# Value projection with its first two products ahead and in the same banks, and linear attention by token halves

## The chip, the cores and the metric

The kernel runs on one core of a Trainium2 chip. The metric is the device time of one execution in microseconds (us); smaller is better. The engines are TensorE (PE, with its weight loads shown apart as PEld), VectorE (DVE), ScalarE (ACT), GpSimd (POOL) and SyncE (SP), which here only issues transfers.

## The reference

Two layers are applied to 512 tokens of 2048 features. Each layer normalises the tokens, makes one wide input projection, runs two groups of heads on slices of it, gates their outputs, and projects back.

```python
D_MODEL, SEQ, DEPTH, CHUNK = 2048, 512, 2, 64
GLA_HEADS, GLA_DK, GLA_DV = 4, 128, 256      # linear attention
ATT_HEADS, ATT_HD = 8, 128                   # chunked attention

def gla_chunk_causal(q, k, v, log_a):        # by head: q, k are 512x128, v is 512x256
    L = cumsum(log_a) inside each chunk; L_end = its last row
    k_dec = k * exp(L_end - L)
    U = einsum('bnchk,bnchv->bnhkv', k_dec, v)          # one 128x256 matrix per chunk
    A = exp(L_end)
    S_c = A_c * S_{c-1} + U_c                           # scan over the 8 chunks
    return einsum('bnchk,bnhkv->bnchv', q * DK**-0.5, S)

def hybrid_layer(x, w_in, w_out, ...):
    h = rmsnorm(x, g_pre)
    gq, gk, gv, gg, ga, aq, ak, av, ag = split_columns(h @ w_in)
    log_a = log_sigmoid(ga @ w_alpha + b_alpha) / 16
    o_gla = rmsnorm(gla_chunk_causal(gq, gk, gv, log_a), per head) * silu(gg)
    o_att = rmsnorm(chunk_band_attention(aq, ak, av, rel_bias), per head) * silu(ag)
    y = concatenate([o_gla, o_att]) @ w_out
    return x + rmsnorm(y, g_post)
```

## The kernel before

**The large products.** The input projection is cut into blocks of 512 columns. The blocks go in pairs (b0, b1), and each pair is multiplied by a scheme of the Strassen kind: seven products P1 to P7 of half-size matrices. A product runs over four chunks c of the inner dimension; one product and one chunk is a `Job`. A job is 12 matmuls of 128x512: each weight is split into a high part `wh` and a low part `wl` (ACT casts `wh` in line L251, DVE makes `wl = src - wh` in L257), and the left operand is split likewise, with three of the four partial products taken, for two halves kk of the chunk and two tiles t of 128 tokens. The weight sources are blocks of 512 KB that arrive in `raw` and `H`; DVE adds or subtracts them for some products (L240 `H += raw`, L243 `raw = H - raw`, L263 `H += src`). All jobs of a layer stand in one list, `stream`; `ahead` prepares them three to five places before they are used, so that loads, casts and differences run beside the matmuls of earlier jobs. A job's matmuls are recorded under line L504 (feature-major pairs under L491, and plain, unpaired blocks, called std, under L380).

**How a pair comes to its four results.** `Pair` holds two PSUM banks X and two banks Y, each a tile of 128x512 per token tile t. In the plain order, `PROD`, the products run P1, P5, middle (P6 and P3 mixed), P7, P2, P4. ACT copies P1, P5 and P6 out of the banks into SBUF tiles `ev` (L430 with a scale per token, L432 without). A result is then a bank combined with such a kept copy by DVE (L445), or a bank alone, scaled and evacuated by ACT (L1397 where the consumer is the value pair). P2 goes into fresh banks Y, and DVE adds the kept P1; P4 continues the sum in X.

In the early form, which the three front pairs of a layer use, P1 and P2 run first. With `seeded`, P2 is added on top of P1 in the same banks X. ACT keeps a copy of P1 before that (L432), writes the copy back into X afterwards (`open`, L439), and once P7 has closed copies X into Y (L517), where P4 then adds up. A function of line L504 called `matmuls` orders a few of the jobs next to such copies by token tile, so that one bank closes ahead of the other (`by_tile`).

**The pairs of a layer.** After the front pairs come `PAIRS`: two pairs of attention queries and keys, then keys and queries of linear attention, then the value pair `PAIRS[3] = (GV0, GV1)`. The value pair is the stage of this study. It has 28 jobs, that is 336 matmuls. After it two std blocks of the output projection follow (the std stage), then an output pair in the early form.

**What runs between the matmuls.** Other work is written as generators in a list `tasks`; `pump` advances it by steps at a rate given to `run`, and `until` advances it as far as something needs. A scheduler then sets the order of instructions on each engine. Near the value pair this work is the last heads of attention and then linear attention. `gla_heads(j, gv)` does heads 2j and 2j+1 in four units, one per head and half of the tokens (4 chunks each), head by head: (2j, first half), (2j, second half), (2j+1, first half), (2j+1, second half). It is started when all of (GV column block j) is done. A unit does: `outer` (8 matmuls of PE per half, L1255, k and v of a chunk; half of the array), `states` (four steps of the scan on DVE, L1274 and L1276, into a tile of slot g9 or g10 by half), `read` (8 matmuls, L1289, half of the array), `norm` (sums of squares on ACT, L1299; the shift on ACT, L556; a power on POOL, L552), `gate` (two instructions of DVE, L1307), and five steps later `turn` (4 transposes on PE, L1317, ACT's scale, L1328, and a split). The names in lists of instructions are tiles: `mm` PSUM banks of large products, `ax` PSUM banks for the rest, `g_...` slots in SBUF, `sm` small columns, `sg` and `bias` the gate tiles.

Of the kernel before, what the change touches and what calls it, by code (L numbers as in the profile page):

```python
# [24 lines left out]
NB_IN = 14  # L25
# [10 lines left out]
def hybrid_trunk(  # L36
# [97 lines left out]
    PAIRS = ((QK01, QK23), (QK45, QK67), (GK, GQ), (GV0, GV1))  # L134
    W23 = (NB_IN + 2, NB_IN + 3)
    C_IN, C_END = (0, 1, 2, 3), (2, 3, 0, 1)
# [37 lines left out]
    class Job:  # L174
# [8 lines left out]
        def load(self):  # L183
            k, c, p, b0, b1 = self.kind, self.c, self.pair, self.b0, self.b1
            end = b0 == W23[0]
# [28 lines left out]
        def bring(self):  # L214
            k, c, p = self.kind, self.c, self.pair
            end = self.b0 == W23[0]
# [4 lines left out]
            if src is None or p.get("direct") or p.get("second") and (name, c) in RESIDENT:  # L221
                return
            until(lambda: (self.l, end, name, c) in made)
            if p.get("second"):
# [41 lines left out]
    for l in range(L):  # L266
# [139 lines left out]
    class Pair:  # L406
        def __init__(self, l, pair, consume, feature_major=False, early=False, end=False, scaled=True, seeded=False, keep=ev,
# [7 lines left out]
            self.by_tile = (("P7", C_IN[-1]), ("P4", C_IN[0]), ("P4", C_IN[-1]), ("P1", C_IN[-1]), ("P2", C_IN[0]))  # L415
# [6 lines left out]
            self.first, *_, self.last = C_END if end else C_IN  # L422
            self.acc, self.keep, self.kept = {}, {}, keep
# [53 lines left out]
        def matmuls(self, job, k, c):  # L477
# [18 lines left out]
            if not self.feature_major:  # L496
                order = [(kk, t) for kk in range(2) for t in range(2)]
                if self.seeded and (k, c) in self.by_tile:
                    order.sort(key=lambda z: z[1])
                for kk, t in order:  # L500
                    tok = slice(kk * 256 + t * P, kk * 256 + (t + 1) * P)
                    ops = ((0, job.wh), (0, job.wl), (1, job.wh))
                    for m, (part, rhs) in enumerate(ops):
                        nc.tensor.matmul(  # L504
# [3 lines left out]
                        )  # L508
            spent.add((self.l, LEFT.get(k), c))

        def run(self, prods, rate=0.0, skip=0, after=None):
            pace = Pace(rate, skip)
            for k, c in prods:
# [5 lines left out]
                ahead(held=int(k == "P7" and c == prods[prods.index((k, self.last)) - 1][1] and self.seeded))  # L519
# [284 lines left out]
    def output_sums(l, chunks):  # L804
# [10 lines left out]
        return make_sums(l, True, ("g0", "g1", "g2", "g3"), parts, chunks)  # L815
# [40 lines left out]
    def layer(l):  # L856
        last = l == L - 1
        if l:
            act_table("silu_and_others")
# [110 lines left out]
        def av_consume(j, h, t, src, comb):  # L970
# [15 lines left out]
            Pair(l, FRONT[0], gate_consume(1), scaled=False, **how),  # L986
            Pair(l, FRONT[1], gate_consume(0), scaled=False, x_bank=2, **how),
            Pair(l, FRONT[2], av_consume, keep=early_kept, close_p1=True, **how),
# [15 lines left out]
        front[0].open(0)  # L1004
# [3 lines left out]
        front[1].open(2)  # L1008
# [6 lines left out]
        front[2].open(0)  # L1015
# [21 lines left out]
        class Head:  # L1037
# [76 lines left out]
            def turn(self):  # L1114
                c, kk = self.hd // 2, self.hd % 2
                if kk == 0:
                    turned[c] = [slot(tag, [2, 512], F32R) for tag in ("g16", "g17")]
# [10 lines left out]
                for half in range(2):  # L1128
# [65 lines left out]
        fast_gemm(l, PAIRS[0], qk_consume(0), rate=2.1, feature_major=True, scaled=False, x_bank=0)  # L1194
        fast_gemm(l, PAIRS[1], qk_consume(1), rate=2.1, feature_major=True, scaled=False, x_bank=2)

# [35 lines left out]

        fast_gemm(l, PAIRS[2], kq_consume, rate=2.1, x_bank=0)

        gla_done = set()
        og = {}

        class Unit:
            def __init__(self, h, p, gv, prev):
                self.h, self.p, self.gv = h, p, gv  # L1240
                self.st = slot(f"g{9 + p}", [4, 256])
                self.prev = prev.st[:, 3, :] if p else None

            def outer(self):
# [6 lines left out]
                for tt in (1, 0):  # L1251
                    for cc in (1, 0):
                        r = slice(cc * 64, (cc + 1) * 64)
                        with tc.issue_after(mm) if mm else nullcontext():
# [3 lines left out]
                            ).ins  # L1258

            def states(self):  # L1260
                h, p = self.h, self.p
                tag = "sg" if (2 * h + p) % 2 else "bias"
# [6 lines left out]
                for q in range(4):  # L1269
                    n = 4 * p + q  # L1270
                    cur = self.st[:, q, :]
# [8 lines left out]
                    prev = cur  # L1280

            def read(self):
                h, p = self.h, self.p
                self.ps_o = aux()
                for tt in range(2):
                    for cc in range(2):
# [4 lines left out]
                            gqT[h // 2][:, h % 2, n * 64 : (n + 1) * 64], self.st[:, q, :],  # L1291
# [20 lines left out]
            def turn(self):  # L1312
# [264 lines left out]
```

## Time and profile before

| quantity | value |
|---|---|
| median of three runs | 1603.68 us (1603.67, 1603.68, 1607.72) |
| profiled execution, its own time | 1604.27 us |
| span of the profile | 1601.9 us |
| mean granted TensorE clock | 0.998 |
| read from memory over the span | 393.01 MB |
| value stage, layer 0 and layer 1 | 534.7 to 625.1 us, and 1327.3 to 1417.4 us |
| std stage up to the end of its second half, layer 0 and layer 1 | 625.1 to 681.3 us, and 1417.4 to 1474.0 us |

The span is what the profiler saw of the core; the execution's own time holds 2.37 us more around it. Rows of the profile have the engine, the line of the kernel, the operation, the tiles written and read, and the time; "idle" names what the engine waited for just before. A matmul's recorded duration overlaps its neighbour's, so the distance between the starts of two matmuls is what one costs.

### The profile page before, as it was taken

To read this page: it belongs to the slowest core of one execution; us is meant where nothing else is said; L and a number is where in the kernel's file an instruction comes from. 1 tells how busy PE (TensorE), PEld (TensorE's weight loads), DVE (VectorE), ACT (ScalarE), POOL (GpSimd) and SP (SyncE) were. 2 spreads that over 40 slices of the span, in tenths; PEclk is the share of its full clock that TensorE was granted. 3 is DMA by queue.
4 is the path that set the end of the run, shared out by engine and by line. 5 is a ranking of instruction groups with operands and counts; after the bars stand their busy time and mean duration, and the time that the engine had idled before them with its cause. 6 is when DMAs were issued, how large, how long until landed. Compare 5 with 4: busy or idle time off the path is not lost.

```text
span 1601.9 us, 24514 instructions
## 1 busy us (share of the span) xinstructions
PE 1588.1 (99%) x8818; PEld 1353.9 (85%) x8818; DVE 1258.1 (79%) x1580; ACT 924.1 (58%) x1534; POOL 189.1 (12%) x302
## 2 busy tenths in 40 slices
PE   9999999999999999999999999999999999999997
PEld 6787889999988887788887888899999888777886
DVE  6888887786877876778868989768778778866886
ACT  8565544456676544555685556445666765355543
POOL 1131000001101101310312100000000011013110
PEclk9999999999999999999999999999999999999999
DMA  9999966858868698799868899668588677979995
GB/s 373 358 337 347 337 220 247 306 188 288 296 216 282 219 345 302 274 376 335 346 241 333 305 345 334 228 228 306 187 312 281 223 263 248 352 241 351 367 330 214
DMA packets 150616, 467.82 MB, mean 292 GB/s; under 512 B 16492, under 2 KB 35956, under 8 KB 150496
## 3 DMA queue, kind: packets, MB, share of 16 engines
q1 hardware_dynamic: 127232, 385.79, 67.7%
q0 software_dynamic: 22688, 79.53, 13.0%
q8 instruction: 69, 1.13, 0.3%
q10 hardware_dynamic: 576, 0.95, 0.2%
q14 instruction: 51, 0.42, 0.1%
HBM read 393.01 MB, written 72.11 MB: 290 GB/s over the span
## 4 chain that ended last, share of the span: by engine, by line
PE 92%; issue 3%; DMA 2%; DVE 1%; POOL 1%; ACT 1%; SPq 0%; POOLq 0%; DVEq 0%
PE mm L504 49%; PE mm L491 20%; PE mm L380 11%; PE ax L1089 2%; PE ax L504 1%; PE ax L1072 1%; PE ax L1255 1%; PE ax L1289 1%; DMA raw<-in_w_dram 1%; DMA H<-in_w_dram 1%; PE ax L1051 1%; PE ax L1052 1%; PE ax L1050 1%; PE ax L687 0%; DVE wl L257 0%
## 5 line engine op out<-in xcount | busy, mean ns | idle before, releaser
L251 ACT CAST wh<-raw 128x1024 fp32r<-128x1024 f32 x256 | 269.3, 1053 | 234.0 <-PE mm L504 97.3
L257 DVE TENSOR_TENSOR wl<-raw,wh 128x1024 fp32r<-128x1024 f32 x256 | 312.5, 1221 | 114.9 <-PE mm L504 36.2
L251 ACT CAST wh<-H 128x1024 fp32r<-128x1024 f32 x239 | 251.1, 1053 | 211.7 <-PE mm L504 88.7
L257 DVE TENSOR_TENSOR wl<-H,wh 128x1024 fp32r<-128x1024 f32 (+1 forms) x241 | 292.9, 1217 | 91.1 <-PE mm L504 36.5
L504 PE MATMUL mm<-wh,sa 128*128 128x512 f32 x1088 | 345.2, 392 | 0.1
L504 PE MATMUL mm<-wh,g 128*128 128x512 f32 x832 | 258.1, 389 | 0.0
L504 PEld LDWEIGHTS mm<-wh,sa 128*128 128x128 f32 x1088 | 203.2, 188 | 43.3 <-issue 1.5
L491 PE MATMUL mm<-sa,wh 128*128 128x256 f32 x1280 | 235.9, 285 | 0.0
L504 PE MATMUL mm<-wh,a 128*128 128x512 f32 x704 | 228.8, 396 | 2.2 <-ACT a L113 0.9
L504 PE MATMUL mm<-wl,sa 128*128 128x512 f32 x544 | 212.6, 391 | 0.0
L240 DVE TENSOR_TENSOR H<-H,raw 128x1024 f32<-128x1024 f32 x160 | 194.3, 1220 | 17.5 <-DMA raw<-in_w_dram 9.4
L491 PEld LDWEIGHTS mm<-sa,wh 128*128 128x128 f32 x1280 | 199.4, 192 | 0.3
L504 PEld LDWEIGHTS mm<-wh,g 128*128 128x128 f32 x832 | 156.2, 188 | 32.3
L491 PE MATMUL mm<-sa,wl 128*128 128x256 f32 x640 | 181.0, 283 | 0.0
L504 PE MATMUL mm<-wl,g 128*128 128x512 f32 x416 | 162.3, 390 | 1.1 <-DVE wl L257 1.1
L504 PEld LDWEIGHTS mm<-wh,a 128*128 128x128 f32 x704 | 131.6, 188 | 35.4 <-issue 4.9
L504 PE MATMUL mm<-wl,a 128*128 128x512 f32 x352 | 137.9, 393 | 0.6 <-DVE wl L257 0.5
L491 PEld LDWEIGHTS mm<-sa,wl 128*128 128x128 f32 x640 | 122.3, 191 | 0.1
L504 PEld LDWEIGHTS mm<-wl,sa 128*128 128x128 f32 x544 | 102.2, 188 | 21.3 <-DVE wl L257 0.3
L552 POOL TENSOR_TENSOR sm<-sm,cst 128x4 f32<-128x4 f32 (+2 forms) x40 | 59.4, 1486 | 321.6 <-DVE sm L1449 128.0
L491 PE MATMUL mm<-a,wh 128*128 128x256 f32 x512 | 94.4, 285 | 0.0
L504 PEld LDWEIGHTS mm<-wl,g 128*128 128x128 f32 x416 | 78.1, 188 | 18.9 <-DVE wl L257 2.6
(208 smaller groups left out, 2272.0 us busy)
## 6 DMA issues: line engine op xcount, KB each, us to landing
raw<-in_w_dram SPq DMA_DIRECT2D x352, 512.0 KB, 5.5
sa<-S SPq DMA_DIRECT2D x128, 512.0 KB, 4.7
H<-in_w_dram SPq DMA_DIRECT2D x63, 512.0 KB, 5.6
S<-g POOLq DMA_DIRECT2D x32, 512.0 KB, 6.4
g<-S SPq DMA_DIRECT2D x32, 512.0 KB, 5.2
sa<-A SPq DMA_DIRECT2D x32, 512.0 KB, 6.1
oS<-g POOLq DMA_DIRECT2D x32, 512.0 KB, 5.8
sa<-oS SPq DMA_DIRECT2D x32, 512.0 KB, 5.0
```

The lines of the kernel that those rows point to most:

```text
L240: nc.vector.tensor_tensor(out=h, in0=h, in1=r, op=ALU.add)
L251: last_cast[0] = nc.scalar.copy(self.wh, src).ins
L257: last_low[0] = nc.vector.tensor_tensor(out=self.wl[:, kk, :], in0=self.src[:, kk, :], in1=self.wh[:, kk, :].bitcast(F32), op=ALU.subtract ...
L380: mm = nc.tensor.matmul(pss[o], a[:, part, t], rhs[:, kk, :], start=(i == 0 and kk == 0 and m == 0), stop=(i == n - 1 and kk == 1 and m == 2),
L491: nc.tensor.matmul(dst, lhs[:, kk, f], a[:, part, tok], start=(fresh and kk == 0 and m == 0 and ft % 2 == 0), stop=(c == self.last and kk ...
L504: nc.tensor.matmul(out_ps[t], a[:, part, tok], rhs[:, kk, :], start=(fresh and kk == 0 and m == 0), stop=(c == self.last and kk == 1 and m ...
L552: return nc.gpsimd.tensor_tensor(out=out_r, in0=v, in1=mhalf[:, : v.shape[-1]], op=ALU.pow).ins
L1050: nc.tensor.matmul(ps[:, :n], self.qh[:, t], self.kh[:, :n], start=True, stop=False)
L1051: nc.tensor.matmul(ps[:, :n], self.qh[:, t], self.kl[:, :n], start=False, stop=False)
L1052: nc.tensor.matmul(ps[:, :n], self.ql[:, t], self.kh[:, :n], start=False, stop=True)
L1072: nc.tensor.transpose(ps[:, j * P : (j + 1) * P], self.prob[i][:, j * P : (j + 1) * P], ident)
L1089: nc.tensor.matmul(o, self.pt[i][:, j * P : (j + 1) * P], av[hd // 4, j // 2][:, j % 2, (hd % 4) * P : (hd % 4 + 1) * P], start=(j == 0), ...
```

## The change

- The value pair takes the early, seeded form: P1 and P2 first, P2 added in P1's banks; then P5, middle, P7, P4. It is split in two calls of `run` with `open` between. P4 needs its lower block of b0 again, so four more weight blocks of 512 KB are loaded per layer. The result (0, 0) of the pair, which DVE made from two tiles, is now evacuated by ACT.
- Linear attention no longer goes head by head. As soon as one of the pair's four results (column block j, token half h) is complete, `gla_heads` is started for the two heads of j and this half alone. The results come in the order (0,0), (1,0), (1,1), (0,1). The state at the end of the first half of each head is kept in `ends`, a slot of its own (g3), and the state tiles g9 and g10 alternate by the order of issue.
- The slots of the four results are new, result (0, 0) needs only the first attention head to be done, and `early_sums` waits in addition until the states of all eight units are issued.
- The counts that change over the whole program: 8 more block loads (`raw`, 352 to 360), the additions of L240 160 to 168 and those of L263 32 to 24, DVE's combinations of L445 20 to 16, ACT's evacuations of L1397 4 to 8, scaled copies of L430 32 to 28, plain copies of L432 64 to 68, writes back into a bank of L439 8 to 12, and copies from bank to bank of L517 12 to 16. PE runs the same instructions in another order.

The diff also has a whole second form of the output projection, `paired_out`, with `by_bank` and everything under `paired`, `W01` and `OUT`. It runs only for layers in `PAIRED`, which is empty, so `flip` is 0 and none of it is built. It is left out here.

```diff
         for b0, b1 in PAIRS:
-            pr = {"early": False}
-            stream += [Job(l, k, c, b0, b1, pr) for k, c in PROD]
+            pr = {"early": b0 == GV0}
+            order = early_head(C_IN) + early_rest(C_IN) if pr["early"] else PROD
+            stream += [Job(l, k, c, b0, b1, pr) for k, c in order]
...
-        gla_done = set()
-        og = {}
+        og, issued = {}, {"outer": 0, "states": 0}
+        ends = slot("g3", [4, 256])
 
         class Unit:
-            def __init__(self, h, p, gv, prev):
-                self.h, self.p, self.gv = h, p, gv
-                self.st = slot(f"g{9 + p}", [4, 256])
-                self.prev = prev.st[:, 3, :] if p else None
+            def __init__(self, h, p, gv):
+                self.h, self.p, self.gv, self.i = h, p, gv, issued["outer"]
+                st = slot(f"g{9 + self.i % 2}", [4, 256])
+                self.st = [st[:, q, :] for q in range(4)]
+                if p == 0:
+                    self.st[3] = ends[:, h, :]
+                self.prev = ends[:, h, :] if p else None
...
-        def gla_heads(j, gv):
+        def gla_heads(specs):
             units = []
 
             def new(k):
-                h, p = 2 * j + k // 2, k % 2
-                units.append(Unit(h, p, gv, units[-1] if p else None))
+                h, p = specs[k]
+                units.append(Unit(h, p, [gv[h // 2, z] if (h // 2, z) in gv else None for z in range(2)]))
                 units[-1].outer()
...
-            for k in range(4):
-                if k < 3:
+            for k in range(len(specs)):
+                more = k < len(specs) - 1
+                if more:
                     new(k + 1)
...
         def early_sums():
             while not {(p, h) for p in range(2) for h in (2, 3)} <= set(og):
                 yield
-            yield from output_sums(l, (2,3,))
+            while not paired and issued["states"] < 8:
+                yield
+            yield from output_sums(l, (2, 3))
...
-        GV = {1: ("g4", "g5"), 0: ("g0", "g1")}
+        GV = {(0, 0): "g2", (1, 0): "g4", (1, 1): "g5", (0, 1): "g0"}
...
-                until(lambda: 4 in heads_done)
-                gv[j, h] = slot(GV[j][h], [2, 512])
+                until(lambda: (4 if j or h else 0) in heads_done)
+                gv[j, h] = slot(GV[j, h], [2, 512])
...
-            if h and t:
-                heads = gla_heads(j, [gv[j, p] for p in range(2)])
-                tasks.append(heads if j else beside(heads, early_sums(), 3))
-
-
-        fast_gemm(l, PAIRS[3], gv_consume, rate=4, after=fetch_operands, x_bank=2)
+            if t:
+                heads = gla_heads([(2 * j, h), (2 * j + 1, h)])
+                tasks.append(beside(heads, early_sums(), 3) if (j, h) == (0, 1) else heads)
+
+        values = Pair(l, PAIRS[3], gv_consume, early=True, seeded=True, x_bank=flip ^ 2)
+        values.run(early_head(C_IN), rate=4, after=fetch_operands)
+        values.open(flip ^ 2)
+        values.run(early_rest(C_IN), rate=4, after=fetch_operands)
```

In the order of instructions the two programs are the same up to the value pair of layer 0, and again in the stages behind the std stage; the same differences stand in layer 1. Two places show them.

**PE, inside linear attention.** Before, the last `outer` of column block 1 and the next `read` (both on half of the array) stand side by side near the end of the value pair. L504 rows are matmuls of the large product, L1255 is `outer`, L1289 is `read`.

```order
L504 MATMUL mm_5835<-wl_6183,a_46_374 128x512
L1255 MATMUL ax_6272<-g_1176_6084,g_1066_5576 128x256
L1255 MATMUL ax_6271<-g_1176_6084,g_1066_5576 128x256
L1255 MATMUL ax_6272<-g_1176_6084,g_1066_5576 128x256
L1255 MATMUL ax_6271<-g_1176_6084,g_1066_5576 128x256
L1289 MATMUL ax_6278<-g_1200_6204,g_1016_5341 64x256 x4
L504 MATMUL mm_5835<-wh_6166,a_46_374 128x512
L504 MATMUL mm_5715<-wh_6186,sa_6188 128x512
```

After, the reads of the first two units stand in pieces among the matmuls of the middle products (L517 is the large product there, L1320 is `read`; `g_1098` is `ends`).

```order
L517 MATMUL mm_5910<-wh_5931,sa_5933 128x512
L1320 MATMUL ax_5977<-g_1147_5935,g_1015_5340 64x256 x3
L1320 MATMUL ax_5977<-g_1098_5715,g_1015_5340 64x256
L1320 MATMUL ax_6018<-g_1151_5949,g_1015_5340 64x256 x2
L517 MATMUL mm_5910<-wl_5969,sa_5933 128x512
L517 MATMUL mm_5910<-wh_5931,sa_5933 128x512
L517 MATMUL mm_5911<-wh_5931,sa_5933 128x512
L517 MATMUL mm_5911<-wl_5969,sa_5933 128x512
L1320 MATMUL ax_6018<-g_1151_5949,g_1015_5340 64x256
L517 MATMUL mm_5911<-wh_5931,sa_5933 128x512
L1320 MATMUL ax_6018<-g_1098_5715,g_1015_5340 64x256
L517 MATMUL mm_5910<-wh_5931,sa_5933 128x512
```

Counted over the whole program, unbroken stretches of `outer` and `read` rows between two full-size matmuls are 24 before and 32 after; per layer two of the eight units move from the std stage into the value stage.

**ACT, at the turn from the last-but-one product to P4 of the value pair.** Before, ACT has the casts of P2 and P4 and the steps of linear attention (`norm` L1299 and L556, `turn` L1328) there.

```order
L251 CAST wh_6186<-H_5572 128x1024
L251 CAST wh_6226<-H_5607 128x1024
L1299 ACTIVATE t_1210_6243,sm_6241<-ax_6230 128x256
L1299 ACTIVATE t_1211_6245,sm_6241<-ax_6230 128x256
L556 ACTIVATE sm_6247<-sm_6241,cst 128x2
L251 CAST wh_6264<-H_5638 128x1024
L251 CAST wh_6297<-H_5668 128x1024
```

After, it also has the two copies from X to Y (L541) between the casts of P4 (L254), ahead of the `norm` of two units (L1330, L580).

```order
L254 CAST wh_6309<-H_5607 128x1024
L541 COPY mm_5912<-mm_5910 128x512
L254 CAST wh_6390<-H_5638 128x1024
L541 COPY mm_5913<-mm_5911 128x512
L1330 ACTIVATE t_1242_6336,sm_6334<-ax_6323 128x256
L1330 ACTIVATE t_1243_6338,sm_6334<-ax_6323 128x256
L580 ACTIVATE sm_6340<-sm_6334,cst 128x2
L1330 ACTIVATE t_1250_6368,sm_6366<-ax_6361 128x256
L1330 ACTIVATE t_1251_6370,sm_6366<-ax_6361 128x256
L254 CAST wh_6397<-H_5668 128x1024
L580 ACTIVATE sm_6372<-sm_6366,cst 128x2
```

P4's first matmuls in each bank Y now stand behind the copy into that bank, and the second copy stands behind the cast `wh_6390`.

Where a line of the kernel before has moved in the kernel after, the pairs that matter are: L504 and L517 (large product), L1255 and L1284 (`outer`), L1289 and L1320 (`read`), L1317 and L1348 (transposes), L1299 and L1330, L556 and L580, L552 and L576, L1307 and L1338 (`norm` and `gate`), L432 and L443, L439 and L450, L517 and L541, L445 and L456, L1397 and L1438 (copies and evacuations).

More of the change, by code (lines that the diff above doesn't have):

```diff
@@ L422, in __init__ @@
             self.first, *_, self.last = C_END if end else C_IN
+            self.by_tile = [(k, self.last) for k in ("P7", "P4", "P1")] + [(k, self.first) for k in ("P4", "P2")]
             self.acc, self.keep, self.kept = {}, {}, keep
@@ L475, in operand, with matmuls @@
             return S_on[self.l, LEFT[k], c]
-        def matmuls(self, job, k, c):
+        def matmuls(self, job, k, c, only=None):
             a = self.operand(job, k, c)
@@ L499, in matmuls @@
                     order.sort(key=lambda z: z[1])
+                if only is not None:
+                    order = [z for z in order if z[1] == only]
                 for kk, t in order:
@@ L508, in matmuls, with by_bank @@
                         )
+                self.closing = mm.ins
             spent.add((self.l, LEFT.get(k), c))
+        def by_bank(self, prods, evac):
+            jobs = [take(self.l, self.b0, k, c) for k, c in prods]
+            closing = None
+            for t in range(2):
+                for job, (k, c) in zip(jobs, prods):
+                    with tc.issue_after(closing) if closing else nullcontext():
+                        self.matmuls(job, k, c, only=t)
+                closing = self.closing
+                evac(t, self.acc[self.target[k]][t])
         def run(self, prods, rate=0.0, skip=0, after=None):
@@ L518, in run @@
                     last_evac[0] = seeds[0]
-                ahead(held=int(k == "P7" and c == prods[prods.index((k, self.last)) - 1][1] and self.seeded))
+                ahead(held=int(self.seeded and (k, c) == ("P7", (C_END if self.end else C_IN)[2])))
                 if c == self.last:
@@ L857, in layer @@
         last = l == L - 1
+        paired = l in PAIRED
+        flip = 2 * (sum(z < l for z in PAIRED) % 2)
         if l:
@@ L1127, in turn @@
                 ks = slice(kk * 256, (kk + 1) * 256)
-                for half in range(2):
+                for half in range(1 if paired else 2):
                     z = turned[c][half]
@@ L1258, in outer @@
                             ).ins
+                issued["outer"] += 1
             def states(self):
                 h, p = self.h, self.p
-                tag = "sg" if (2 * h + p) % 2 else "bias"
+                tag = "sg" if self.i % 2 else "bias"
                 self.sg = tmp.tile([P, 2, 256], F32, tag=tag, name=nm(tag), bufs=2)
@@ L1463, in finish @@
         def finish(pair, xs):
-            p4 = next(i for i, z in enumerate(stream) if z.l == l and z.b0 == W23[0] and z.kind == "P4")
-            while done["low"] < p4 + 4:
+            at, n = (("P4", 2) if last else ("P7", 2)) if paired else ("P4", 4)
+            first = next(i for i, z in enumerate(stream) if z.l == l and z.b0 == W23[0] and z.kind == at)
+            while done["low"] < first + n:
                 yield
```

116 lines of the change are left out of this document (94 added, 22 removed).

## The prediction

> **What bounds the kernel now.** I read the page's shares first, then the stages in which the change lies, then PE's waits, and last single stretches of the timeline.
>
> ```profile
> PE 1588.1 (99%) x8818; PEld 1353.9 (85%) x8818; DVE 1258.1 (79%) x1580; ACT 924.1 (58%) x1534; POOL 189.1 (12%) x302
> PEclk9999999999999999999999999999999999999999
> PE 92%; issue 3%; DMA 2%; DVE 1%; POOL 1%; ACT 1%; SPq 0%; POOLq 0%; DVEq 0%
> ```
>
> PE is busy for 99% of the span at an undisturbed clock, and the chain that ended last is PE for 92%. An average can hide a stage with another limit, so the table of stretches comes next: the value stage and the std stage of layer 0, the output pair that follows, and the first two of layer 1.
>
> ```profile
> core 0: us, PE busy (x) PEld busy (x) DVE busy (x) ACT busy (x) POOL busy (x), PEclk, DMA share, GB/s
> 534.70:625.10 90.40, 90.40 (x440) 71.40 (x439) 71.78 (x95) 43.62 (x75) 10.75 (x10) 1.00 0.80 290
> 625.10:681.30 56.20, 56.20 (x281) 42.64 (x281) 36.41 (x63) 27.97 (x63) 17.35 (x28) 1.00 0.79 278
> 681.30:777.00 95.70, 95.70 (x424) 79.23 (x423) 80.66 (x87) 51.05 (x70) 12.80 (x14) 1.00 0.96 363
> 1327.30:1417.40 90.10, 90.10 (x440) 71.10 (x439) 71.47 (x95) 43.53 (x75) 10.40 (x10) 1.00 0.81 290
> 1417.40:1474.00 56.60, 56.60 (x283) 43.00 (x282) 36.86 (x64) 28.04 (x64) 17.87 (x29) 1.00 0.81 289
> ```
>
> In all five PE is busy the whole time. DVE has 79% in the value stage (71.78 of 90.40), 65% in the std stage; ACT about half. So time is set by what PE runs and by the gaps between its matmuls. The waits of PE over the whole program, and of its weight loads for the two copies that matter here:
>
> ```profile
> PE mm L504 <- DVE wl L257: 1.6, 4, 0.5
> PE ax L827 <- DVE t L824: 1.2, 1, 1.2
> PE mm L504 <- ACT a L113: 0.9, 1, 0.9
> PE mm L504 <- ACT pc L432: 0.8, 1, 0.8
> PEld mm L504 <- ACT pc L432: 1.5, 2, 1.2
> PEld mm L504 <- ACT mm L517: 0.5, 1, 0.5
> ```
>
> The columns are total us, times, longest. Waits come to a few us of 1602. There is almost nothing that better overlap could win, and a change that leaves PE its instructions can move the time only by what lies between them or by a new wait.
>
> **The change part by part.** PE runs the same instructions, kind by kind, in both programs. Two of eight units per layer move from the std stage to the value stage, with all of their steps.
>
> *Half-array stretches.* In the timeline (start, duration, engine, line, tiles) one `outer` among full matmuls, and an `outer` with a `read` right behind it, look like this:
>
> ```profile
> 595.02 0.39 PE L504 MATMUL mm<-wl,a 128*128 128x512 f32 x1
> 595.25 0.39 PE L504 MATMUL mm<-wh,a 128*128 128x512 f32 x1
> 595.57 1.13 PE L1255 MATMUL ax<-g,g 64*128 64x256 f32 x8
> 596.63 0.50 PE L504 MATMUL mm<-wh,a 128*128 128x512 f32 x1
> 596.97 0.40 PE L504 MATMUL mm<-wl,a 128*128 128x512 f32 x1
> ...
> 615.46 0.39 PE L504 MATMUL mm<-wh,sa 128*128 128x512 f32 x1
> 615.77 1.13 PE L1255 MATMUL ax<-g,g 64*128 64x256 f32 x8
> 616.84 1.08 PE L1289 MATMUL ax<-g,g 128*64 128x256 f32 x8
> 617.85 0.50 PE L504 MATMUL mm<-wh,sa 128*128 128x512 f32 x1
> ```
>
> From start to start a full matmul costs 0.23 (595.02 to 595.25). The last one ahead of the `outer` costs 0.32 and the first one behind it 0.34: going to half of the array and back costs 0.09 + 0.11 = 0.20 beyond the work. The work itself costs the same joined or apart: 1.06 alone, 1.07 and 1.01 joined. So a joint stretch saves one 0.20, and each stretch that the change splits off adds 0.20. Stretches go from 24 to 32, eight more: 8 x 0.20 = 1.6 us. Some of the new ones are single reads, which no row of before shows; if each edge of these cost twice as much, 8 x 0.40 = 3.2. I take 0.25 each, near the row: **+2.0**.
>
> *The moved units.* A unit's PE work goes along: 2 x (1.06 + 1.01) = 4.1 us per layer and the transposes. Since both stages have PE busy throughout, the value stage becomes longer and the std stage shorter by the same: 0. Were the std stage held by something else, its end would stay and the value stage's growth would be lost time; 56.20 of 56.20 excludes that.
>
> *Copies between banks.* The groups concerned:
>
> ```profile
> L445 DVE SCALAR_TENSOR_TENSOR g<-mm,norm,ev 128x512 f32<-128x512 f32 x20 | 14.9, 746 | 1.1 <-PE mm L504 0.5 <-ACT mm L517 0.5
> L1397 ACT ACTIVATE g<-mm,norm 128x512 f32<-128x512 f32 x4 | 2.7, 684 | 0.1
> L517 ACT COPY mm<-mm 128x512 f32<-128x512 f32 x12 | 6.9, 579 | 13.7 <-PE mm L504 13.7
> L439 ACT COPY mm<-ev 128x512 f32<-128x512 f32 x8 | 4.4, 592 | 0.0
> L432 ACT COPY ev<-mm 128x512 f32<-128x512 f32 x64 | 37.4, 584 | 27.4 <-PE mm L504 14.9 <-PE mm L491 12.3
> L430 ACT ACTIVATE ev<-mm,norm 128x512 f32<-128x512 f32 x32 | 22.0, 686 | 9.0 <-PE mm L504 8.7
> ```
>
> DVE loses four combinations, 4 x 0.746 = 3.0 us, and its `H +=` merely moves from P2 to P4; off the path, 0. ACT gets four each of 0.584, 0.592, 0.579 and 0.684 and loses four of 0.686: 9.8 - 2.7 = 7.0 us over both layers. Hidden by the matmuls of the neighbouring jobs, as ACT has 46.8 us of each value stage free (90.40 - 43.62). Three joins are new, where PE can be late: P2 behind the copy of P1, P5's successors behind the write-back, P4 behind the copy from X to Y. The six front pairs already do this: their weight loads wait 1.5 + 0.5 us in all, 0.33 a pair, so two more pairs cost at most 0.7 by these rows and nothing at the other end. P4's second copy stands behind the cast that waits for DVE's `H +=`, with most of a job of matmuls in the first bank to cover it. If that cover went, each 1.2 us of DVE would be paid. I take **+0.3**.
>
> *Four more weight blocks a layer.*
>
> ```profile
> raw<-in_w_dram SPq DMA_DIRECT2D x352, 512.0 KB, 5.5
> ```
>
> A block lands 5.5 us after its issue, and jobs load three to five places ahead, of 12 x 0.23 = 2.8 us each. The value stage moves 290 x 90.4 = 26.2 MB; with 2.1 MB more it would be at 313 GB/s, and the output pair runs at 363 with PE busy throughout: 0. SP issues eight more of 352; no wait of PE for SP's transfers of weights is in the list.
>
> *The gate.* The one chain that stands closer to PE is `read`, `norm`, the power on POOL, `gate`, `turn`. Before, in the value stage, and a power alone at 642; then all powers (shortest, median, longest, in ns), and the transposes:
>
> ```profile
> 602.67 1.08 PE L1289 MATMUL ax<-g,g 128*64 128x256 f32 x8
> 603.69 0.74 PE L504 MATMUL mm<-wh,a 128*128 128x512 f32 x2
> ...
> 604.84 1.22 DVE L257 TENSOR_TENSOR wl<-H,wh 128x1024 fp32r<-128x1024 f32 x1
> 604.97 1.04 ACT L251 CAST wh<-H 128x1024 fp32r<-128x1024 f32 x1
> 605.14 1.49 POOL L552 TENSOR_TENSOR sm<-sm,cst 128x2 f32<-128x2 f32 x1 [43.97 <-ACT sm L556]
> 606.67 0.88 DVE L1307 SCALAR_TENSOR_TENSOR bias<-ax,sm,bias 128x256 f32<-128x256 f32 x2 [0.61 <-POOL sm L552]
> ...
> 642.39 0.71 POOL L552 TENSOR_TENSOR sm<-sm,cst 128x2 f32<-128x2 f32 x1 [9.19 <-ACT sm L556]
> L552 POOL TENSOR_TENSOR sm<-sm,cst x40: 550/1073/4617, 346.4 to 1594.5; 128x4 f32<-128x4 f32 x16, 128x2 f32<-128x2 f32 x16, 128x1 f32<-128x1 f32 x8
> L1317 PE MATMUL ax<-cst,sg 128*128 128x128 f32 x32 | 5.4, 272 | 0.0
> ```
>
> From the read's end (603.69) to the gate's (606.67 + 0.88) it is 3.9 us. In PE's new order the matmuls between a unit's last read and its first transposes are 27, 28, 17 and 18 for the first four units of a layer, so 6.2, 6.4, 3.9 (and an `outer`, 1.06) and 4.1 us (and four transposes of 5.4 / 32 = 0.17, so 4.8). The fourth has a cast of 1.04 inside its chain on ACT (the order shows it ahead of `sm_6372`): 3.9 + 1.0 = 4.9 against 4.8, 0.1 late. Lower end 0 (with the power at 0.71). At the upper end a power takes 4.6, 3.1 more than here: 3.2 a layer, 6.4 in all. The row of 605.14 is from this stage, so I stay near it: **+0.5**. Queued behind the late transposes would be the next matmuls of P4, and so everything.
>
> The power's length is worth a look, since DVE is what it runs beside. Started under DVE's difference (604.84 to 606.06), it ended 0.57 after that; alone it took 0.71. The Trainium skill, "SBUF — State Buffer", section "Who interferes with whom", says that a DVE instruction with two inputs in SBUF contends with a GpSimd instruction that reads SBUF, by an exclusive lock in which the second fully blocks; the two rows agree with it. By that rule a power in the denser DVE stage may wait for a whole DVE instruction of 1.22 each time; by the median row it costs nothing that the sum doesn't hold.
>
> *Sum.* 1604.27 (the profiled execution: span 1601.9 and 2.37 around it) + 2.0 + 0.3 + 0.5 = 1607.1. That execution was 0.59 above the median of the runs, 1603.68, so **1606.5** on the scale of the medians. A difference under 0.3%, 4.8 us, is about what cannot be told from no change: between 1598.9 and 1608.5.
>
> **Rivals.**
>
> *The gate comes late (slower).* The price is the upper end above: 1606.5 - 0.5 + 6.4 = 1612.4. For it: two more units run where DVE is at 79%, and powers of up to 4.6 exist. Against it: the median is 1.07, and the first three units have 1 us or more to spare. It decides beyond 1608.5 when the fourth unit's power takes more than 2.7 us in both layers (1.25 late each, 0.1 of it at 1.49).
>
> *The extra blocks are the bound (slower).* If the stage were held by transfers, 2.1 MB at 363 GB/s is 5.8 us a layer: 1606.5 + 11.6 = 1618. Against it: 290 GB/s now, and the stage that shows 363 keeps PE busy.
>
> *Fewer waits (faster).* With four combinations of DVE less, the waits for `wl` (1.6) could go while the new stretches cost as little as one would lose: 1603.7 - 1.6 = 1602.1. More isn't there to be had, since PE's waits listed above are 4.5 us over the whole program and lie mostly elsewhere.
>
> *It comes to nothing.* The same PE instructions, the edges hidden: 1603.7 to 1604.3.
>
> **How the numbers follow.** The sum's case, 1604.5 to 1608.5: 0.58. Nothing: 0.16. Fewer waits: 0.10, of which 0.03 below 1598.9, by something that I don't see. Late gate: 0.13. Transfers: 0.03. So faster 0.03, same 0.58 + 0.16 + 0.07 = 0.81, slower 0.16. The range goes from 1602.5, near the faster rival's, to 1611, most of the way to the late gate: what is left out is some 0.05 below, 0.08 of the late gate and 0.03 of the transfers.
>
> **What the profile after would show.** Right: PE still busy throughout both stages; the value stage about 5 us longer and the std stage 5 shorter; L541 x16, L450 x12 into a bank from `ev`, L1438 x8, L456 x16, 360 loads of `raw`; waits of PE for L443 and L541 under 1 us; some 0.3 at each edge of the split reads. Wrong: PE or its weight loads waiting for L1338 behind a long L576, or for `wl` L260 near P4; a stage with the DMA share near 1 and PE idle; single reads among matmuls that cost far more than 0.2 beyond their work, which would make the first term wrong.

## The result, and the profile after

The changed kernel is slower: 1617.88 us against 1604.56 in the comparison made with it, ratio 1.0078, 95% interval 1.0056 to 1.0099. Timed again on another occasion (`a0_again` below) it was 1613.42 against 1605.98, ratio 1.0046, 1.0033 to 1.0059. It was forecast at 1606.5, no change. The profiled execution has a span of 1616.1 us, 14.2 more than before.

The page's shares after, which answer to the same lines of before:

```profile
PE 1596.7 (99%) x8818; PEld 1356.2 (84%) x8818; DVE 1255.1 (78%) x1576; ACT 930.1 (58%) x1546; POOL 177.3 (11%) x302
PEclk9999999999999999999999999999999999999999
PE 81%; DMA 8%; issue 6%; DVE 2%; ACT 2%; POOL 1%; SPq 0%; POOLq 0%; DVEq 0%; ACTq 0%
```

The same number of PE instructions takes 8.6 us more of busy time (1588.1 before), and the rest of the 14.2 is idle time. The chain that ended last is no longer PE alone: transfers hold 8% of it (2% before). The value stage and the std stage of layer 0, cut at their first and last work:

```profile
core 0: us, PE busy (x) PEld busy (x) DVE busy (x) ACT busy (x) POOL busy (x), PEclk, DMA share, GB/s
536.35:633.60 97.25, 97.25 (x480) 75.17 (x478) 77.72 (x109) 51.66 (x94) 11.64 (x13) 1.00 0.82 308
633.60:685.90 52.30, 52.30 (x244) 40.29 (x244) 28.39 (x46) 23.07 (x51) 13.17 (x23) 1.00 0.80 299
```

PE is still busy throughout both. The value stage went from 90.40 to 97.25 us, the std stage from 56.20 to 52.30. The second window ends three large matmuls later than that of before; to the same matmul it is 51.75. So the two moved units went over, and 2.4 us came on top during which PE waits for nothing that the profile shows. (At 681.3 us, where the table of before ends the std stage, only the first of its two blocks is done. The second runs to 703.7 before and 708.9 after, in the stretch that the prediction calls the output pair.) PE's waits over the program:

```profile
PE mm L391 <- ACT wh L254: 2.6, 2, 2.2
PE mm L517 <- DVE wl L260: 2.4, 5, 0.6
PE mm L517 <- ACT a L113: 1.3, 2, 0.8
PE mm L517 <- ACT pc L443: 1.3, 1, 1.3
...
PE mm L517 <- ACT mm L541: 0.3, 1, 0.3
PE mm L517 <- DMA sa<-A: 0.2, 1, 0.2
```

New is the first row, a plain (std) matmul that waits for the cast of its weights. The rest grew by less than 1 us each; L541 has 0.3.

To see where the time is lost I set the starts of the 7488 large matmuls (the same ones in the same order in all these programs) against those of before. Large matmul 2676 stands shortly ahead of the value pair of layer 0, 3200 near the end of linear attention there, 3450 behind the second std block; 4350 to 6436 brings nothing; 6960 and 7200 are in layer 1 what 3200 and 3450 are in layer 0. The columns are what each stretch of profiled execution took more than before, in us; the runs are explained below.

| kernel | up to 2676 | 2676 to 3200 | 3200 to 3450 | 3450 to 6436 | 6436 to 6960 | 6960 to the end | all |
|---|---|---|---|---|---|---|---|
| after | 1.65 | 2.40 | 1.16 | 1.18 | 3.04 | 4.84 | 14.27 |
| a0_again | 1.00 | 3.34 | 4.34 | 0.64 | 2.76 | 1.94 | 14.02 |
| e1_head_by_head | -0.47 | 5.38 | 7.62 | 0.93 | 6.65 | 6.21 | 26.32 |
| e3_whole_reads | 0.87 | 1.25 | 0.00 | 0.26 | 0.65 | 0.00 | 3.03 |
| e4_sums_not_held | 1.20 | 2.71 | 0.81 | 0.63 | 3.98 | 0.83 | 10.16 |
| e5_whole_reads_not_held | 0.34 | 1.59 | 0.82 | 1.21 | 0.40 | 0.82 | 5.18 |
| e6_head_by_head_not_held | 0.57 | 5.38 | 0.89 | 0.95 | 5.41 | 0.80 | 14.00 |
| e10_before_held | 0.25 | 0.16 | 8.33 | 2.50 | 0.16 | 5.21 | 16.61 |
| e11_before_held_pool | 0.78 | 0.17 | 15.46 | 6.42 | 0.17 | 15.52 | 38.51 |
| e12_whole_reads_pool | 0.04 | 1.99 | 2.45 | 1.37 | 0.77 | 1.70 | 8.32 |

The first column is code that no edit touches; it differs by up to 2 us from one execution to another, and I take the fourth for the same kind, except in e10_before_held and e11_before_held_pool. The second and fifth repeat for one kernel to within about 1 us. The third and sixth do not: the two executions of the changed kernel lost 6.0 and 6.3 us there, but in another place each.

Not all of that loss is waiting. Behind a long wait PE also runs slower for a while. In layer 1 of the changed kernel PE stands from 1502.45 to 1504.62; after that the granted clock is lower until 1509.11, and the large matmuls follow each other at 0.43 us instead of 0.23:

```profile
core 0: us, PE busy (x) PEld busy (x) DVE busy (x) ACT busy (x) POOL busy (x), PEclk, DMA share, GB/s
1502.45:1504.62 2.17, 0.00 (x1) 0.00 (x0) 1.79 (x4) 1.61 (x3) 1.07 (x2) 1.00 0.95 355
1504.62:1509.11 4.49, 4.27 (x11) 3.06 (x12) 3.48 (x3) 2.97 (x4) 0.53 (x1) 0.62 1.04 372
1509.11:1512.00 2.89, 2.89 (x14) 2.38 (x13) 2.34 (x3) 2.15 (x5) 0.00 (x0) 1.00 0.98 347
```

Of the 4.84 us of the sixth column, 2.3 are this wait and about 1.7 the lower clock (eight distances that are 0.2 to 0.28 longer). In the traces of all these runs every wait of PE of 2.1 us or more inside the program has such a stretch of half clock with it, 3.4 us long or a multiple of that (the waits are 2.2 and 2.1 in the two executions of the changed kernel, and 2.9 to 7.8 in e1, e10 and e11). No wait of 1.7 us or less has one.

**The price of half-array stretches.** The timeline of PE in layer 0 after, with the first two units' reads (L1320) among large matmuls:

```profile
574.51 0.61 PE L517 MATMUL mm<-wh,sa 128*128 128x512 f32 x2
575.05 1.51 PE L1320 MATMUL ax<-g,g 128*64 128x256 f32 x12
576.50 0.50 PE L517 MATMUL mm<-wl,sa 128*128 128x512 f32 x1
576.83 0.63 PE L517 MATMUL mm<-wh,sa 128*128 128x512 f32 x2
577.30 0.40 PE L517 MATMUL mm<-wl,sa 128*128 128x512 f32 x1
577.62 0.65 PE L1320 MATMUL ax<-g,g 128*64 128x256 f32 x2
578.20 0.50 PE L517 MATMUL mm<-wh,sa 128*128 128x512 f32 x1
578.63 0.65 PE L1320 MATMUL ax<-g,g 128*64 128x256 f32 x2
579.21 0.51 PE L517 MATMUL mm<-wh,sa 128*128 128x512 f32 x1
579.55 0.39 PE L517 MATMUL mm<-wl,sa 128*128 128x512 f32 x1
```

A read is two records (two passes), so the x8 of a unit's `read` in the lists are four reads. Six reads together take 576.50 - 575.05 = 1.45, so 0.24 each. One read alone takes 578.20 - 577.62 = 0.58. In the trace the records of neighbouring reads start in pairs, 0.007 us apart, one on each half of the array, and the pairs 0.209 apart (0.26 between the first two). A read alone has no partner: its second record starts 0.27 after the first, and the last record of any stretch holds the next large matmul for 0.31 instead of 0.21. A piece of two reads also takes 0.58 in this trace (at 653.55), so a lone read costs as much time as two. With the edges (0.32 and 0.34 instead of 0.23) a lone read costs 0.56 beyond its paired work, a read unit in one piece 0.36, an outer in one piece 0.40. The Trainium skill, "TensorEngine Tiling (Array Packing)", section "Tiling Modes", says that tiles operate in parallel and that a change of mode drains the engine. The starts 0.007 us apart agree with the first; the longer distances at the edges, 0.32 and 0.34, would fit the second.

Summed over every start-to-start distance in and at the edges of these stretches (less 0.227 for a large matmul and 0.108 for a half-array record), the two layers cost 5.25 and 5.25 us beyond the work before and 7.78 and 7.97 after: 5.25 us in all. The second and fifth columns of the table together hold 5.44.

### The profile page after: what moved, and what is told of

It reads as the page before. It is cut to its first block, busy times and chain, and to the rows that moved or that the text cites. A ratio compares the mean times of both kernels' runs of the same rounds, so it can differ in the third digit from the quotient of the medians.

```text
span 1616.1 us, 24529 instructions
## 1 busy us (share of the span) xinstructions
PE 1596.7 (99%) x8818; PEld 1356.2 (84%) x8818; DVE 1255.1 (78%) x1576; ACT 930.1 (58%) x1546; POOL 177.3 (11%) x302
## 4 chain that ended last, share of the span: by engine, by line
PE 81%; DMA 8%; issue 6%; DVE 2%; ACT 2%; POOL 1%; SPq 0%; POOLq 0%; DVEq 0%; ACTq 0%
PE mm L517 45%; PE mm L502 20%; PE mm L391 6%; DMA raw<-in_w_dram 4%; PE ax L1115 2%; PE ax L517 1%; PE ax L1098 1%; DMA H<-in_w_dram 1%; DVE wl L260 1%; DMA oS<-g 1%; DMA g<-in_x_dram 1%; PE ax L1077 1%; PE ax L1078 1%; DMA sa<-A 1%; ACT wh L254 1%
## 5 line engine op out<-in xcount | busy, mean ns | idle before, releaser
L254 ACT CAST wh<-raw 128x1024 fp32r<-128x1024 f32 x256 | 269.2, 1052 | 228.3 <-PE mm L517 92.6
L254 ACT CAST wh<-H 128x1024 fp32r<-128x1024 f32 x239 | 250.6, 1052 | 205.7 <-PE mm L517 73.9
L517 PE MATMUL mm<-wh,sa 128*128 128x512 f32 x1088 | 346.8, 393 | 0.6 <-ACT mm L541 0.3
L517 PE MATMUL mm<-wh,g 128*128 128x512 f32 x832 | 258.5, 389 | 0.3 <-DMA g<-S 0.3
L517 PEld LDWEIGHTS mm<-wh,sa 128*128 128x128 f32 x1088 | 203.1, 188 | 47.7 <-issue 4.1
L517 PE MATMUL mm<-wh,a 128*128 128x512 f32 x704 | 226.9, 395 | 3.6 <-ACT a L113 1.3
L243 DVE TENSOR_TENSOR H<-H,raw 128x1024 f32<-128x1024 f32 x168 | 204.3, 1222 | 28.6 <-DMA raw<-in_w_dram 21.0
L517 PE MATMUL mm<-wl,sa 128*128 128x512 f32 x544 | 213.4, 392 | 0.0
L517 PEld LDWEIGHTS mm<-wh,g 128*128 128x128 f32 x832 | 156.2, 188 | 33.0 <-ACT t L113 0.7
L517 PE MATMUL mm<-wl,g 128*128 128x512 f32 x416 | 162.6, 391 | 1.4 <-DVE wl L260 1.3
L517 PEld LDWEIGHTS mm<-wh,a 128*128 128x128 f32 x704 | 131.4, 188 | 35.1 <-issue 2.5
L517 PE MATMUL mm<-wl,a 128*128 128x512 f32 x352 | 138.1, 394 | 1.1 <-DVE wl L260 1.1
L517 PEld LDWEIGHTS mm<-wl,sa 128*128 128x128 f32 x544 | 102.2, 188 | 22.6 <-issue 1.4
L517 PEld LDWEIGHTS mm<-wl,g 128*128 128x128 f32 x416 | 78.1, 188 | 19.7 <-DVE wl L260 3.6
L391 PE MATMUL mm<-wh,a 128*128 128x512 f32 x256 | 85.9, 399 | 2.6 <-ACT wh L254 2.6
```

Source lines behind the costliest of these rows:

```text
L243: nc.vector.tensor_tensor(out=h, in0=h, in1=r, op=ALU.add)
L254: last_cast[0] = nc.scalar.copy(self.wh, src).ins
L391: mm = nc.tensor.matmul(pss[o], a[:, part, t], rhs[:, kk, :], start=(i == 0 and kk == 0 and m == 0), stop=(i == n - 1 and kk == 1 and m == 2),
L517: mm = nc.tensor.matmul(out_ps[t], a[:, part, tok], rhs[:, kk, :], start=(fresh and kk == 0 and m == 0), stop=(c == self.last and kk == 1 ...
```

## The experiments

**a0_again**, the changed kernel without an edit. 

> The changed kernel once more, unchanged. Its first profile is 14.2 us longer than that of before: 6.0 us in the value and std stages of both layers, 4.8 us at the end of layer 1's second std block (PE waited 2.2 us for a cast whose weights came late), 3.4 us in code that the change doesn't touch (1.65 in the first 160 us). Visits theory: the 6.0 us repeat to 0.2 us, since PE's order is fixed. Late-sums theory: the loss behind the second std block repeats as well (3 to 5 us in one layer or both); if it was chance it is gone. The 1.65 us of the start should be chance. Ratio to before 1.006 to 1.010.

Measured: 1.0046 (1.0033 to 1.0059), below the expected range; six executions from 1610.5 to 1617.7, of which the profiled one is the longest. The half-array stretches repeat, 7.97 and 7.98; the stages lost 6.1 us (3.34 + 2.76) against 5.4 (2.40 + 3.04) in the first profile. The loss behind the second std blocks was there again in this profile, 4.3 and 1.9, but the shorter executions leave no room for it: 7.4 us over before by the medians, of which 5.5 are half-array stretches. So it seems to come and go with the execution; no trace of a short one exists. The start gave 1.00.

**e3_whole_reads**, the four reads of a unit chained from the last state to the first, so that all are ready at once:

```diff
-                for tt in range(2):
-                    for cc in range(2):
+                mm = None
+                for tt in (1, 0):
+                    for cc in (1, 0):
...
-                        nc.tensor.matmul(
+                        with tc.issue_after(mm) if mm else nullcontext():
+                            mm = nc.tensor.matmul(
...
```

> The changed kernel with one edit: the four reads of a unit are chained from the last state to the first, so that all four stand together; 24 half-array stretches, no single read. Visits theory: stretches of one read cost 0.56 us beyond their work and the edges 0.36 to 0.40; the value and std stages come out 3.3 us per layer shorter than in the changed kernel, 6.5 us in all (ratio 1.0035 to 1.0045 if the late weights stay, 0.999 to 1.001 if not). Rival, the gate chain or DVE is what holds PE: later reads make it longer or leave it as it is (1.007 or more).

Measured: 1.0012 (1.0003 to 1.002), 1607.9 against 1605.98, which is 5.5 us less than a0_again beside it. Half-array stretches 5.14 and 5.13. In the timeline the same reads stand in two whole pieces of 1.01 and 1.02 us (575.19 to 576.20, 577.80 to 578.82):

```profile
575.19 1.08 PE L1322 MATMUL ax<-g,g 128*64 128x256 f32 x8
576.20 0.74 PE L517 MATMUL mm<-wh,sa 128*128 128x512 f32 x2
...
577.80 1.08 PE L1322 MATMUL ax<-g,g 128*64 128x256 f32 x8
578.82 0.73 PE L517 MATMUL mm<-wh,sa 128*128 128x512 f32 x2
```

So the split reads are the part of the loss that every execution has. The stages came out 4.2 us shorter than in a0_again (1.25 + 0.65), less than the 6.5 expected: the edit also delays the gates, and there the late gate does appear (transposes L1350 wait 0.5 for L1340); this, not the stretches, is most of the 1.25 and 0.65 us that its stages are still over before. Behind the second std blocks this profile lost nothing.

**e4_sums_not_held**, the first output sums without the wait for all eight units' states:

```diff
-            while not paired and issued["states"] < 8:
-                yield
-            yield from output_sums(l, (2, 3))
+            yield from output_sums(l, (2, 3), ("g1", "g2", "g6", "g7"))
```

> The changed kernel with the first output sums no longer waiting until all eight units' states are issued (their staging slots are g1, g2, g6, g7 instead of g0 to g3, which hold values and end states). Late-sums theory: the first sums start about 5 us earlier and spread out, so the late weights behind layer 1's second std block cost 2 to 5 us less (ratio 1.0045 to 1.0065). Rival, the time of heads 2 and 3 sets the sums: less than 1 us changes. PE's half-array stretches are as in the changed kernel, so the 6 us of the stages stay.

Measured: 1.0045 (1.0033 to 1.0057), the same as a0_again. The last store of the first sums stands at large matmul 3210 and 6954 (3236 and 6985 in the changed kernel, 3188 and 6925 before), so the edit takes back about half of their delay. Its profile lost 1.6 us behind the second std blocks instead of 6, but the medians show no gain, as the rival has it, though the sums did come earlier: inconclusive on this loss, and the hold alone is not what costs the changed kernel its time.

**e5_whole_reads_not_held**, both edits. 

> Whole reads as in e3_whole_reads and the first output sums not held as in e4_sums_not_held. Late-sums theory: half-array stretches cost 5.1 us per layer as in e3_whole_reads (7.8 to 8.0 in the changed kernel, 5.25 in before), and no late weights in any run, so the median comes 0.5 to 1.5 us under e3_whole_reads: ratio 0.999 to 1.0008. Rival, the hold doesn't matter: 1.0012 again.

Measured: 1.0028 (1.0016 to 1.004). A miss: not better than e3_whole_reads, if anything worse, although the first sums' last store comes earlier (3210 and 6954, against 3234 and 6979 there).

**e1_head_by_head**, the new pair with the old order of heads:

```diff
-            if t:
-                heads = gla_heads([(2 * j, h), (2 * j + 1, h)])
-                tasks.append(beside(heads, early_sums(), 3) if (j, h) == (0, 1) else heads)
+            if h and t:
+                heads = gla_heads([(2 * j, 0), (2 * j, 1), (2 * j + 1, 0), (2 * j + 1, 1)])
+                tasks.append(heads if j else beside(heads, early_sums(), 3))
```

> The new value pair stays; linear attention goes head by head again, started when a column block is complete. Visits theory: 28 half-array stretches, 14 per layer, of which two are split outers and one a split read, so about 1 us per layer more than before; order theory: heads 2 and 3 are complete early again, the first output sums start 10 us earlier, no late weights, total within 3 us of before (ratio 0.999 to 1.002). Rival, the pair itself (four more blocks, copies between banks) is the loss: ratio stays 1.005 or more.

Measured: 1.0151 (1.0137 to 1.0164). A clear miss, and the order of heads does not restore the time. I had overlooked that the hold stays: the eighth unit's states come last in this order, so that the first sums' last store stood at large matmul 3264 and 7010. The loss behind the second std blocks is 7.6 and 6.2 us.

**e6_head_by_head_not_held**, the same with the hold taken out (as in e4, and the state passed on from unit to unit instead of through `ends`). 

> e1_head_by_head (new value pair, heads one after the other) with the first output sums not held until all states are issued, and without the slot for end states. Late-sums theory: e1_head_by_head lost 13.8 us behind the second std blocks of both layers because the hold put the first sums' last store at matmul 3264 and 7010 (before: 3188 and 6925); now it lies near before's and that loss is under 2 us. Its half-array stretches stay at 28 as in e1_head_by_head, 8.4 to 8.9 us per layer, 6.5 us more than before in all, and late transposes cost up to 4; ratio 1.004 to 1.007. Rival, the new pair itself makes the loss: ratio 1.010 or more.

Measured: 1.0074 (1.0061 to 1.0087), slightly above the expected range. The last store of the first sums is at 3186 and 6930, and the loss behind the std blocks falls from 13.8 to 1.7 us. The stages stay 5.4 us a layer over before: half-array stretches 8.79 and 7.94, and transposes that are late by about 1.9 a layer. So with the new pair the old order of heads costs more than the token halves (1.0045 in e4_sums_not_held, also without the hold).

**e10_before_held**, the kernel before with only the hold added:

```diff
-        og = {}
+        og, issued = {}, {"states": 0}
...
+                issued["states"] += 1
...
+            while issued["states"] < 8:
+                yield
             yield from output_sums(l, (2,3,))
```

> The kernel before with one edit: its first output sums wait until the states of all eight units are issued, as the change has it. The value pair and linear attention's order stay as before. Late-sums theory: the first sums' last store moves from matmul 3188 toward 3264, and PE waits for late weights behind the second std block: 3 to 14 us over both layers, ratio 1.002 to 1.009, of which under 1 us is from two more half-array stretches. Rival, the transfers hide it and the loss in e1_head_by_head was of the pair: ratio 0.9995 to 1.001.

Measured: 1.0090 (1.0076 to 1.0103). One wait among the tasks, with nothing of the value pair changed, costs 14.7 us by the medians (two more half-array stretches are 0.4 of it). The last store of the first sums is at 3263 and 7008. PE's waits, where before had none on L251:

```profile
PE mm L380 <- ACT wh L251: 5.0, 2, 3.5
PE mm L504 <- DVE wl L257: 2.3, 6, 0.7
PE mm L380 <- DVE wl L257: 2.2, 2, 1.1
```

That late sums make PE wait behind the second std block is thereby shown by itself.

**e11_before_held_pool** and **e12_whole_reads_pool**: what in the sums is late. The weight cast stands in order on ACT. In the changed kernel at the end of the second std block of layer 1:

```profile
1497.28 1.05 ACT L254 CAST wh<-raw 128x1024 fp32r<-128x1024 f32 x1 [7.37 <-DMA raw<-in_w_dram]
1497.97 0.69 DVE L789 TENSOR_TENSOR t<-t,t 128x512 f32<-128x512 f32 x1 [5.57 <-DMA t<-fg]
1498.69 0.62 ACT L113 CAST g<-t 128x512 fp32r<-128x512 f32 x1 [0.36 <-DVE t L789]
...
1503.01 0.62 ACT L113 CAST g<-t 128x512 fp32r<-128x512 f32 x1 [0.58 <-DVE t L789]
1503.53 1.04 ACT L254 CAST wh<-raw 128x1024 fp32r<-128x1024 f32 x1
...
1504.62 0.73 PE L391 MATMUL mm<-wh,a 128*128 128x512 f32 x2 [2.17 <-ACT wh L254]
```

Between two weight casts ACT does four copies for the sums (L113), each behind a sum of DVE (L789), the first of which waited 5.57 for its input; the first of the two casts had waited 7.37 for its weights. Two suspects then, ACT's order and full transfers. The edit, on e10_before_held and on e3_whole_reads:

```diff
-                split(op[:, 0, :], op[:, 1, :], {"S1": a22, "S3": a21, "S2": a22, "S4": a12}[name])
+                src = {"S1": a22, "S3": a21, "S2": a22, "S4": a12}[name]
+                if end:
+                    nc.gpsimd.tensor_copy(op[:, 0, :], src)
+                    nc.vector.tensor_tensor(out=op[:, 1, :], in0=src, in1=op[:, 0, :].bitcast(F32), op=ALU.subtract)
+                else:
+                    split(op[:, 0, :], op[:, 1, :], src)
```

> e10_before_held with one more edit: the high part of each output sum is copied by GpSimd instead of ScalarE. In e10_before_held (14.7 us over before) and in the changed kernel the weight cast that PE waits for stands on ScalarE behind such copies, which wait for a sum's input to land. ScalarE-order theory: with the copies off ScalarE the casts go ahead and most of the 14.7 us is gone: ratio 0.999 to 1.003. Rival, the weights themselves land late because transfers are full: ratio stays 1.006 or more.

> e3_whole_reads (the changed kernel with the four reads of a unit in one piece, 1.0012) with the output sums' high parts copied by GpSimd. ScalarE-order theory: executions of e3_whole_reads between 1604.7 and 1609.5 differ by late casts; these go and the median comes to that of before: ratio 0.999 to 1.0005. Rival: GpSimd's copy is slower than ScalarE's and the sums' stores come later, so nothing is won or up to 3 us are lost: 1.001 to 1.003.

Measured: e11 1.0236 (1.0221 to 1.0252), e12 1.0059 (1.0047 to 1.0072). Both are slower than the kernels they start from; e11 came out as its rival has it, e12 beyond both ranges. PE's waits in e11:

```profile
PE mm L504 <- DMA sa<-oS: 16.9, 4, 7.8
PE mm L380 <- DVE wl L257: 7.3, 4, 3.2
...
PE mm L380 <- ACT wh L251: 1.1, 2, 0.6
```

The wait of std matmuls for ACT's cast fell from 5.0 to 1.1 in e11 (e12 has none, but neither had e3_whole_reads); but GpSimd's copy takes 1.07 us (0.92 in e12) where ACT's takes 0.62, the sums came later still (last store of the first at 3276 and 7021 in e11, 3264 and 7009 in e12), and now PE waits for the sums themselves to come back from memory (`sa<-oS`, 16.9 us in e11, 3.1 in e12). By their times these runs are inconclusive between the two suspects.

The traces separate the two for single waits, since a weight block and its cast share a semaphore. The block of the late cast above was issued at 1492.22 and had landed at 1501.26. A cast begun then would have ended at about 1502.3 (an estimate from the 1.04 of the row), and PE was ready at 1502.45; but ACT began it at 1503.53, behind its copies. The other three waits of this kind in the two profiles of the changed kernel are alike: the cast begins 2.1 to 2.3 us behind the landing, and by the same estimate PE would not have waited without that. In e10_before_held the cast begins 2.1 and 1.2 us behind it, and without that 1.3 and 0.2 us of the waits of 3.5 and 1.5 would be left. In e1_head_by_head the cast begins 0.1 us behind the landing, and the block landed 13.9 and 13.4 us after its issue (9.0 to 11.3 in the changed kernel, whose median is 5.6). So in the changed kernel slow transfers used up the slack, and ACT's order made PE wait; in e1 the transfers alone did.

## Why the prediction was wrong

- **Half-array stretches: the term that was mis-sized.** Forecast +2.0 (eight stretches at 0.25, bounds 0.20 to 0.40 each); measured +5.25 with the forecast count, 24 to 32, so 0.66 each. The 0.20 was read from a joined and an unjoined stretch and counted only the two edges; the last record's 0.10 I had left within "the work itself". And I took the order's rows of single reads for smaller pieces of the same work, bounded at twice the edges, where a lone read loses its partner on the other half of the array: 0.56. The new order has ten lone reads, five in each layer; single reads that cost far more than 0.2 were the sign that the prediction named for this term being wrong. e3_whole_reads, which only puts them together, takes the term away again. Of the 7.4 us that the changed kernel is over before in the second comparison, this term is the greater part.
- **The sums: a step that was missing.** The value pair computes P2 ahead of P7, so result (1, 1), which P7 completes, comes four jobs later. Heads 2 and 3, whose sums are the first of the output projection, are ready for them later; the scaling behind their last transposes is at 631.52 before and 641.88 after (two units' rows in one):

```profile
631.52 0.84 ACT L1328 ACTIVATE t<-ax,gcol 128x256 f32<-128x256 f32 x2 [1.25 <-PE ax L1317]
```

```profile
641.88 1.57 ACT L1359 ACTIVATE t<-ax,gcol 128x256 f32<-128x256 f32 x4 [1.44 <-PE ax L1348]
```

  The diff showed the hold in `early_sums`, and I priced neither that nor the later heads; of the 48 large matmuls by which the last store moves in layer 0 (3188 to 3236), e4_sums_not_held gives back 26 for the hold. That "both stages have PE busy throughout" was true and didn't cover it, since the price falls due behind the second std block, 70 us further on. That such sums cost time when late is shown (e10, e1 against e6). That they cost the changed kernel the 6 us of its two profiles is argued, not shown: PE waits there for the same cast behind the same copies, but storing the sums earlier gained nothing by the medians (e4, e5), and e3_whole_reads stores them as late as the changed kernel (3234 and 6979) and its profile lost nothing there. So the sums have some slack (in e3_whole_reads 46 and 54 large matmuls later than before cost nothing); that the changed kernel is near its end would fit, but isn't shown. Why the loss varies between executions stays open, and with it why the first comparison has 13.3 us between the medians and the second 7.4.
- **Copies between banks, +0.3.** The copies weren't late (L541 0.3 in the list). The term's size came out by luck: at the turn to P4 PE waited instead for P4's operand (`sa<-A`): 0.2 in this execution, 0.5 in a0_again, the longest in the trace 1.1 (e4_sums_not_held). That is about the size foreseen, by another cause.
- **Four more blocks, 0.** Right: 308 GB/s in the value stage with PE busy throughout.
- **The gate, +0.5, and its rival.** It didn't come late in the changed kernel: PE's waits have no row for the transposes (L1348), as before (L1317). It did in e3_whole_reads and e6. And the power that the prediction calls alone (642.39, 0.71) wasn't alone; DVE ran beside it, reading its large operands from SBUF (`g`) and from PSUM (`ax`):

```profile
641.86 2.02 DVE L1276 SCALAR_TENSOR_TENSOR g<-g,a_end,ax 128x256 f32<-128x256 f32 x4
```

  The row of 605.14 and this one therefore compare two kinds of neighbour, not one with none.
- **The moved units, 0.** Right: to the same matmul the value stage became 6.8 us longer and the std stage 4.4 shorter; the 2.4 between them are about the stretches' 2.5 in that layer.

The range, 1602.5 to 1611, was bounded by rivals near the edit only; 1613.4 and 1617.9 lie beyond it.

No version here beats the kernel before: the best, e3_whole_reads, is 0.12% slower than it.

## What to carry to other kernels

When PE is full, count not only how many instructions are moved but in what company they stand: matmuls on half of the array are cheap in pairs and in one piece, so tie those that belong together, chained behind the one that is ready last. And when results are produced in another order, follow each of them to its last consumer: a result that comes later may be paid for two stages on, while the stage of the change shows no wait. A wait of PE that grows long costs more than its length, as the granted clock showed here.

## What the runs showed of the hardware

A matmul on 64 columns of the array runs beside its neighbour on the other 64 (starts 0.007 us apart); alone it takes as long as two do together, 0.58 until the next large matmul, and the entry to and the exit from half-array work cost some 0.3 in edges and tail. Behind waits of PE of 2.1 us and more the granted clock was at half for 3.4 us or a multiple, with large matmuls 0.43 us apart; behind waits of 1.7 us and less it was not. One added wait among the background tasks (e10_before_held) cost 14.7 us of 1606, nearly 1%, without any engine getting more work.
